# A decoder layer in one core: two late steps of the first MLP half by seven products, and copies of weight sums on another queue

## The chip, the cores and the metric

The kernel runs on one core of a Trainium2 chip. Its time is the device time in microseconds of one execution of the whole layer. Several runs of a kernel are made, and their median is the number that is compared.

## The reference

One layer of a decoder trunk over 1024 tokens of width 1024, with 16 learned tokens put in front of them and dropped at the end. All arrays are float32.

```
u = rmsnorm(h) @ w_in                          # 1024 -> 2048, four pieces of 512
y_lru = rg_lru(conv4(x_lru)) * gelu(g_lru)     # gated linear recurrence
y_cc  = silu(layernorm(conv31(v * sigmoid(g))))
h = h + concat(rmsnorm(y_lru), rmsnorm(y_cc)) @ w_out
m = rmsnorm(h) @ w_mlp_up                      # 1024 -> 4096
h = h + square(relu(m)) @ w_mlp_down           # 4096 -> 1024
out = rmsnorm(h)
```

Most of the matrix products are the MLP's, and it is what the change is about.

## The kernel before

**Products.** A float32 matrix is held as two parts, hi and lo (the rounded value and the rest), both of the type fp32r. Each product is three: hi·hi + hi·lo + lo·hi. For each weight block of 128x1024 the raw block is loaded (512 KB), ACT casts hi (line 313), and DVE subtracts to get lo (line 322). There are 16 buffers for weight blocks in the three forms together, so a load can start only when a block that was used before has been set free.

**Halves.** The tokens are taken in two halves of 512. The mixer of the first half runs first. Then comes the MLP of the first half, with the mixer of the second half worked in between its products; then the MLP of the second half.

**The MLP of the first half** goes in 16 groups of 256 hidden features. `mlp_up` makes 48 matmuls of 128x512 for a group (two blocks of `w_mlp_up`), relu and square on ACT and a subtraction on DVE; `mlp_down` makes 48 more for the group before it (two blocks of `w_mlp_down`), whose sums DVE adds to the residual out of PSUM. Two groups are called a step here; there are eight steps, and the down product of one takes 96 matmuls.

**The MLP of the second half** goes in eight steps of 512 features, each by a scheme of seven products in place of eight (`up_fast`, `down_fast`): the operands are cut in two by two quarters, and sums and differences of the quarters are multiplied. A step's down product takes 84 matmuls in place of 96. For it the activations have to be added and subtracted on DVE, with a further split in hi and lo of each sum. Seven weight blocks go in: three are loaded from the weights, and four are sums of quarters.

**The sums of weights** are made in DRAM by DMAs alone (`weight_sums`). For each step and kind (up, down) there are four blocks, made by four copies from the weights and four DMAs that add onto them. All eight are issued on POOL's queue. There are 15 sums, in the order (step 0, up), (step 0, down), (step 1, up) and so on, without (step 7, down); the last step does its down product another way, by `down_last`. The sums are needed only in the second half.

**What sets the order.** The program is recorded first. Each operation has a duration that the planner assumes, and a list scheduler (`Plan`) then sets one fixed order on every engine, by the priority in which operations were recorded; those recorded under `BG` come last. `tick` hangs one DMA of the sums on every sixth microsecond of planned PE work from 40 on, by an `after` that holds in the plan alone: on the chip no instruction waits for it. POOL thus runs its DMAs as soon as the data that they read are there and POOL gets to them. SP's queue carries x, all weight loads and the stores, in the planned order; where a load must wait for a free buffer, all that stands behind it on SP waits too. DVE and ACT take their instructions in order as well.

**Names of buffers.** `w` is a weight block (raw, hi or lo), `s` a 128x512 slot of activations, `ws_up` and `ws_down` are the sums in DRAM, `mm`, `cv` and `tr` are PSUM banks. In the rows of the order, `ws_up_3_0` is block 0 of the sum for step 3, up.

**Places that the prediction speaks of.** At the start, SP loads x. POOL meanwhile loads blocks of `w_in` with a DMA that adds onto a block that holds minus hi, which makes lo without DVE (`load_split`, line 548). Near 480 us the mixer of the second half and the first half's MLP share PE. From about 560 to 690 us steps 5, 6 and 7 of the first half run; after that the second half's MLP begins. The function that holds the loop over the groups is shown with the others:

Of the kernel before, what the change touches and what calls it, by code (L numbers as in the profile page):

```python
# [14 lines left out]
AF = mybir.ActivationFunctionType  # L15
# [5 lines left out]
KD = D // P  # L21
# [10 lines left out]
NG = NF // 2  # L32
# [30 lines left out]

TABLES = {AF.Sigmoid: 1, AF.Tanh: 2, AF.Exp: 3, AF.Sqrt: 4, AF.Gelu_apprx_tanh: 5, AF.Silu: 6}

G_FIN = 8
G_OUT = 11


class Buf:  # L70
# [204 lines left out]
def hymba_kernel(  # L275
# [25 lines left out]
    def act(o, i, func, scale=1.0, bias=None, accum=None):  # L301
        n = width(i)
        dur = 0.01 + 0.000916 * n + (0.0 if func == AF.Copy else 0.042)
        dur += 0.09 * len(refs(bias, accum)) + 0.115 * len(refs(scale))

        def fn():
            kw = {}
            if bias is not None:
                kw["bias"] = val(bias)
            if accum is not None:  # L310
                kw["accum_out"] = val(accum)
            if func == AF.Copy and isinstance(scale, float) and scale == 1.0:
                nc.scalar.copy(val(o), val(i))  # L313
            else:
                nc.scalar.activation(out=val(o), in_=val(i), func=func, scale=val(scale), **kw)  # L315
        return pl.add("act", dur, fn, refs(i, scale, bias), refs(o, accum), TABLES.get(func))
# [63 lines left out]
    def mms(o, pairs, start=True, stop=True):  # L380

        n = width(o)
        dur = len(pairs) * per_matmul(pairs[0][0], n)
        last = len(pairs) - 1

        def fn():
            for k, (a, b) in enumerate(pairs):
                nc.tensor.matmul(val(o), val(a), val(b), start=start and k == 0,  # L388
                                 stop=stop and k == last)
        rd = [r for p in pairs for r in p]  # L390
        op = pl.add("pe", dur, fn, rd, [o])
        tick(op)
        return op
# [11 lines left out]
    def dma(o, src, nbytes, q="sp", after=()):  # L405
        e = nc.sync if q == "sp" else nc.gpsimd
        return pl.add(q, 0.47 if q == "sp" else 1.02, lambda: e.dma_start(val(o), src), [], [o],
                      nbytes=nbytes, after=after)
# [8 lines left out]
    def dma_pool(o, src, nbytes, add=False, after=()):  # L417
        kw = {"accum_op": ALU.add} if add else {}
        if add and isinstance(src, Ref):
            kw["max_dma_last_dim"] = 1024  # L420
        return pl.add("pool", 1.02, lambda: nc.gpsimd.dma_start(val(o), val(src), **kw),  # L421
                      refs(src) + ([o] if add else []), [o], nbytes=nbytes, after=after)
# [4 lines left out]
    def slot(dt=F32, w=512):  # L427
        return pl.buf("s", dt)[:, 0:w]
# [4 lines left out]
    def bank(tag):  # L433
        return pl.buf(tag)[:, 0:512]
# [93 lines left out]
    def load_cols(w, col):  # L528

        raws = []  # L530
        for h in range(2):
            r = wtile(F32)
            dma(r.view(k4), w[h * 512:(h + 1) * 512, col:col + 256].rearrange("(k p) n -> p k n", p=P),
                1 << 19)
            raws.append(r)
        return raws
# [25 lines left out]
    def prep_win(raws, eng="dve"):  # L562

        return by_column_tile([split_w(r, eng) for r in raws])
# [44 lines left out]
    w_up2 = w_up.rearrange("l d n -> (l d) n")  # L609
# [13 lines left out]
    def weight_sums(q, kind):  # L623

        blk, k, (x, y, z, v) = ((up_block, k4, ((1, 0), (1, 1), (0, 0), (0, 1))) if kind == "up"
                                else (dn_block, k2, ((0, 1), (0, 0), (1, 1), (1, 0))))
        t = [pl.fixed(dr.tile([P, 1024], F32, name=f"ws_{kind}_{q}_{n}"))[:, 0:1024] for n in range(4)]
        n = 1 << 19
        for o, src in ((t[0], x), (t[1], z), (t[2], x), (t[3], v)):
            yield lambda after, o=o, src=src: dma_pool(o.view(k), blk(q, *src), n, after=after)  # L630
        yield lambda after: dma_pool(t[0].view(k), blk(q, *y), n, True, after)
        yield lambda after: dma_pool(t[2].view(k), blk(q, *z), n, True, after)
        yield lambda after: dma_pool(t[1], t[0], n, True, after)
        wsum[q, kind] = t
        yield lambda after: dma_pool(t[3], t[1], n, True, after)

    sums = [(q, kind) for q in range(NG // 2) for kind in ("up", "down")][:-1]

    pace = {"sums": (f for s in sums for f in weight_sums(*s)), "pe": 0.0, "next": SUM_FROM}

# [334 lines left out]
    for c0 in (0, 2):  # L975
        ws = split_win(c0 * P)
# [129 lines left out]
    def mlp_up(gs, u2T, cuts):  # L1106
        ws, bs, hids = {}, {}, []
        for g in gs:
            ws[g] = prep_win(load_cols(w_up2, g * 256))
            bs[g] = [bank("mm"), bank("mm")]  # L1110
        for c0, c1 in cuts:
            for g in gs:
                for j in range(2):
                    pairs = []
                    for k in range(KD):
                        hi, lo = u2T[k]
                        whi, wlo = ws[g][j][k]
                        pairs += [(whi, hi[:, c0:c1]), (whi, lo[:, c0:c1]), (wlo, hi[:, c0:c1])]
                    mms(bs[g][j][:, c0:c1], pairs)
        for g in gs:  # L1120
            hid = []
            for j in range(2):
                r, hi, lo = slot(), slot(F32R), slot(F32R)
                act(r, bs[g][j], AF.Relu)
                act(hi, r, AF.Square)
                act(r, r, AF.Square)
                tt(lo, r, hi.f32, ALU.subtract)
                hid.append((hi, lo))
            hids.append(hid)
        return hids  # L1130

    def mlp_down(gs, hids, hv, done=None, last=False):
        ws = []
        for g in gs:
            for j in range(2):
                r = wtile(F32)
                f0 = (2 * g + j) * P
                dma(r, w_dn2[f0:f0 + P, :], 1 << 19)
                ws.append(split_w(r))
        n = len(ws) - 1  # L1140

        def mm(t, b, c0, c1):
            tsl, dsl = slice(t * P, (t + 1) * P), slice(c0, c1)
            for i, ((hhi, hlo), (whi, wlo)) in enumerate(zip(hids, ws)):
                mms(b, [(hhi[:, tsl], whi[:, dsl]), (hhi[:, tsl], wlo[:, dsl]),
                        (hlo[:, tsl], whi[:, dsl])], start=i == 0, stop=i == n)

        for t in range(4):
            if t == 3 and last:
                last_tile(t, hv, lambda *a: mm(3, *a))  # L1150
                break
            for dh in range(2):
                b = bank("mm")
                mm(t, b, dh * 512, (dh + 1) * 512)
                tt(hv[t][dh], b, hv[t][dh], ALU.add)
            if done is not None:
                done(t)
# [185 lines left out]
    def finish(half, hv):  # L1343
        def done(t):
            r = row_rstd(hv, (t,), rstd_fast if half == 1 else rstd_of)
            for h in range(2):
                o = slot()
                if half == 0 or h == 1:
                    stt(o, hv[t][h], r[:, 0:1], gf[h], ALU.mult, ALU.mult)
                else:  # L1350
                    act(o, hv[t][h], AF.Copy, scale=r[:, 0:1])
                    tt(o, o, gf[h], ALU.mult, "pool")
                put(half, t, h, o)
        return done
# [33 lines left out]
        put(1, t, 1, o1)  # L1388
        put(1, t, 0, o0)

    hB = u2B = None
    todo = []
    for g in range(NG):
        if g < 2:
            if g == 0:
                hids = mlp_up((0, 1), u2A, ((0, 256), (256, 512)))
            hid = hids[g]
        else:
            hid, = mlp_up((g,), u2A, ((0, 512),))
        todo.append((g, hid))  # L1400
        if len(todo) > 1:
            gd, hd = todo.pop(0)
            mlp_down((gd,), hd, hA)
        if g == 5:
            for h in range(2):
                s = slot()
                dma(s, norm_final_g[h * 512:(h + 1) * 512].partition_broadcast(P),
                    1 << 18, "pool", after=[pl.ops[-1]])
                gf.append(s)
        if g == G_FIN:  # L1410
            sqB = slot()
            yB = [lru_y(ct, stB[ct]["h"], sqB) for ct in range(NCT)]
            rlB = sumsq_rstd(sqB)
            ycB, rcB = cc_finish(1)
        if g == G_OUT:
            hBt = [pl.buf("c") for _ in range(4)]
            hB = [[t[:, 0:512], t[:, 512:1024]] for t in hBt]
            load_resid(1, hB, ())
            u2B = out_proj(1, yB, ycB, rlB, rcB, hB)
    u2 = u2_blocks(u2B)  # L1420
    hq = up_fast(0, u2)
    gd, hd = todo.pop(0)
    mlp_down((gd,), hd, hA, finish(0, hA))
    for q in range(1, NG // 2):
        nxt = up_fast(q, u2)
        down_fast(q - 1, hq, hB)
# [36 lines left out]
```

## Time and profile before

| | us |
|---|---|
| median of 3 runs | 1024.62 (1024.51 to 1027.83) |
| the profiled execution | 1022.59 |
| its span (first instruction to last) | 1020.8 |
| TensorE busy in the span | 1002.9 (98%) |
| VectorE busy | 833.1 (82%) |
| ScalarE busy | 524.4 (51%) |
| GpSimd busy | 151.7 (15%) |

The profile is of one execution. PE is the TensorE matmul, PEld its weight load (which runs beside it), DVE VectorE, ACT ScalarE, POOL GpSimd, SP SyncE; SPq is the queue of SP, on which instructions only issue DMAs. In a row, "out<-in" names the buffers, then come the shapes and the number of instructions (x). A bracket or a last column gives the idle time of the engine just before, and behind the arrow what ended it. "PEclk" is the share of its full speed at which TensorE's clock ran in the stretch. "DMA share" is the mean busy share of the 16 DMA engines; it may go slightly above 1.

### The profile page before, as it was taken

The numbers are of one execution on the slowest core, as the hardware profiler recorded it, in microseconds if no ns is written. First come the engines' busy times: TensorE is split into PE (matmuls) and PEld (weight loads), VectorE is DVE, ScalarE is ACT, GpSimd is POOL, SyncE is SP. The second block draws the span as 40 slices with busy tenths as digits, with TensorE's granted clock in tenths as the row PEclk, the third lists the DMA queues.
The fourth block names the chain that finished last, engine by engine and source line by source line (L and its number), as shares of the span: only waits on it lengthen the run. The fifth ranks groups of instructions, "written<-read, shape, count | busy, mean of one in ns | idle before, by whom it ended". The sixth has DMA issues, their size and how long they took to land.

```text
span 1020.8 us, 14830 instructions
## 1 busy us (share of the span) xinstructions
PE 1002.9 (98%) x5624; PEld 864.0 (85%) x5624; DVE 833.1 (82%) x1445; ACT 524.4 (51%) x824; POOL 151.7 (15%) x179
## 2 busy tenths in 40 slices
PE   9999999999999999999899999999999999999997
PEld 7888998988797888878778888889988988989985
DVE  6798898698989999999566575577998797897875
ACT  5831045656678333334353373357666656556644
POOL 4324324212200032222222200000000000000001
PEclk9999999999999999999899999999999999999999
DMA  9449999999922299999999952234856565566522
GB/s 310 101 89 229 194 209 206 212 262 247 225 86 82 83 245 275 243 242 218 246 274 269 212 145 83 97 112 143 282 186 191 177 196 186 177 195 189 183 103 83
DMA packets 113240, 191.19 MB, mean 187 GB/s; under 512 B 6668, under 2 KB 73244, under 8 KB 113168
## 3 DMA queue, kind: packets, MB, share of 16 engines
q0 software_dynamic: 50112, 76.39, 35.4%
q1 hardware_dynamic: 63056, 113.85, 34.1%
q8 instruction: 44, 0.72, 0.3%
q14 instruction: 28, 0.23, 0.1%
HBM read 186.02 MB, written 67.11 MB: 248 GB/s over the span
## 4 chain that ended last, share of the span: by engine, by line
PE 85%; DMA 5%; DVE 4%; ACT 3%; issue 1%; SPq 0%; ACTq 0%
PE mm L388 54%; PE mm L373 17%; PE cv L373 8%; PE tr L373 4%; ACT s L315 2%; DMA s<-in_x_dram 1%; DMA w<-in_w_mlp_down_dram 1%; DVE cv L327 1%; DMA w<-in_w_mlp_up_dram 1%; DVE s L322 1%; PE tr L401 1%; DVE w L322 1%; DMA w<-in_w_out_dram 1%; ACT w L313 1%; DMA w<-in_w_in_dram 1%
## 5 line engine op out<-in xcount | busy, mean ns | idle before, releaser
L388 PE MATMUL mm<-s,w 128*128 128x512 f32 (+2 forms) x2016 | 369.5, 343 | 2.3 <-ACT w L313 1.0
L388 PEld LDWEIGHTS mm<-s,w 128*128 128x128 f32 x2016 | 315.7, 189 | 49.0 <-ACT w L313 1.3
L388 PE MATMUL mm<-w,s 128*128 128x512 f32 (+1 forms) x1260 | 299.2, 395 | 4.3 <-DVE s L322 4.3
L313 ACT CAST w<-w 128x1024 fp32r<-128x1024 f32 x193 | 200.0, 1047 | 193.1 <-DMA w<-in_w_mlp_down_dram 62.0
L388 PEld LDWEIGHTS mm<-w,s 128*128 128x128 f32 x1260 | 235.0, 189 | 59.2 <-DVE s L322 5.8
L322 DVE TENSOR_TENSOR w<-w,w 128x1024 fp32r<-128x1024 f32 x193 | 234.9, 1220 | 55.1 <-ACT w L313 54.5
L327 DVE SCALAR_TENSOR_TENSOR cv<-c,prm,cv 128x512 f32<-128x512 f32 x232 | 162.5, 750 | 0.4
L373 PEld LDWEIGHTS mm<-s,w 128*128 128x128 f32 x1152 | 139.2, 188 | 1.4
L373 PE MATMUL mm<-s,w 128*128 128x256 f32 x1152 | 140.3, 281 | 0.0
L322 DVE TENSOR_TENSOR s<-s,s 128x512 fp32r<-128x512 f32 (+4 forms) x183 | 122.3, 686 | 18.0 <-ACT s L315 15.7
L322 DVE TENSOR_TENSOR s<-mm,s 128x512 f32<-128x512 f32 x144 | 97.6, 686 | 38.5 <-PE mm L388 17.8
L315 ACT ACTIVATE s<-s 128x512 f32<-128x512 f32 (+2 forms) x152 | 95.3, 632 | 33.6 <-DVE s L322 30.7
L373 PE MATMUL cv<-w,s 128*128 128x512 f32 x336 | 83.5, 394 | 0.0
L313 ACT CAST s<-s 128x512 fp32r<-128x512 f32 (+2 forms) x83 | 50.6, 622 | 57.8 <-DVE s L322 40.1
L373 PEld LDWEIGHTS cv<-w,s 128*128 128x128 f32 x336 | 62.2, 188 | 13.7
L322 POOL TENSOR_TENSOR s<-s,s 128x512 f32<-128x512 f32 x3 | 4.6, 1541 | 421.8 <-ACT s L315 421.8
L421 POOL DMA_DIRECT2D ws_up<-in_w_mlp_up_dram x48 | 48.5, 1279 | 47.3 <-DMA ws_up<-in_w_mlp_up_dram 47.3
L313 ACT COPY s<-mm 128x512 f32<-128x512 f32 (+2 forms) x48 | 24.4, 513 | 60.2 <-PE mm L373 32.1
L421 POOL DMA_DIRECT2D ws_down<-in_w_mlp_down_dram x42 | 39.6, 1251 | 56.8 <-DMA ws_down<-in_w_mlp_down_dram 56.8
L322 DVE TENSOR_TENSOR c<-mm,c 128x512 f32<-128x512 f32 (+2 forms) x49 | 31.0, 634 | 14.4 <-PE mm L388 14.0
L315 ACT ACTIVATE s<-mm 128x512 f32<-128x512 f32 x40 | 23.7, 594 | 34.0 <-PE mm L388 33.3
L373 PE MATMUL mm<-w,s 128*128 128x512 f32 x168 | 41.1, 393 | 0.0
(133 smaller groups left out, 718.3 us busy)
## 6 DMA issues: line engine op xcount, KB each, us to landing
w<-in_w_mlp_down_dram SPq DMA_DIRECT2D x57, 512.0 KB, 4.3
w<-in_w_mlp_up_dram SPq DMA_DIRECT2D x56, 512.0 KB, 4.8
ws_up<-in_w_mlp_up_dram POOLq DMA_DIRECT2D x48, 512.0 KB, 9.4
ws_down<-in_w_mlp_down_dram POOLq DMA_DIRECT2D x42, 512.0 KB, 9.4
w<-ws_up SPq DMA_DIRECT2D x32, 512.0 KB, 3.9
w<-ws_down SPq DMA_DIRECT2D x28, 512.0 KB, 4.0
w<-in_w_in_dram POOLq DMA_DIRECT2D x24, 512.0 KB, 8.4
ws_up<-ws_up POOLq DMA_DIRECT2D x16, 512.0 KB, 7.8
```

Source lines behind the costliest of these rows:

```text
L313: nc.scalar.copy(val(o), val(i))
L315: nc.scalar.activation(out=val(o), in_=val(i), func=func, scale=val(scale), **kw)
L322: return pl.add(eng, dur, lambda: e.tensor_tensor(out=val(o), in0=val(a), in1=val(b), op=op), refs(a, b), [o])
L327: return pl.add("dve", dur, lambda: nc.vector.scalar_tensor_tensor(out=val(o), in0=val(a), scalar=val(s), in1=val(b), op0=op0, op1=op1), r ...
L373: nc.tensor.matmul(val(p), val(a), val(b), start=start and i == 0 and k == 0, stop=k == len(pairs) - 1, skip_group_check=True)
L388: nc.tensor.matmul(val(o), val(a), val(b), start=start and k == 0, stop=stop and k == last)
L401: nc.tensor.transpose(val(o), val(i), ident.real[:rows, :rows])
L421: return pl.add("pool", 1.02, lambda: nc.gpsimd.dma_start(val(o), val(src), **kw), refs(src) + ([o] if add else []), [o], nbytes=nbytes, a ...
```

## The change

There are four edits.

1. `FAST = (5, 6)`: steps 5 and 6 of the first half take their down product by `down_fast`, as the second half does. Their up product stays at 96 matmuls (`up_blocks`), and its output is evacuated in pieces of 128x256, since `down_fast` needs quarters by tokens.
2. The sums for (step 5, down) and (step 6, down) are made first, since they are now used in the first half.
3. The four copies of each sum go by `dma` (SP's queue) in place of `dma_pool`. The DMAs that add stay on POOL.
4. The loop runs over steps instead of groups. The second half's mixer is finished after step 4 (before: in the middle of step 4, after group 8), and its output projection is made after step 5 (group 11, as before).

```diff
-G_FIN = 8
-G_OUT = 11
+Q_FIN = 4
+Q_OUT = 5
+FAST = (5, 6)
@@ weight_sums
         for o, src in ((t[0], x), (t[1], z), (t[2], x), (t[3], v)):
-            yield lambda after, o=o, src=src: dma_pool(o.view(k), blk(q, *src), n, after=after)
+            yield lambda after, o=o, src=src: dma(o.view(k), blk(q, *src), n, after=after)
         yield lambda after: dma_pool(t[0].view(k), blk(q, *y), n, True, after)
...
-    sums = [(q, kind) for q in range(NG // 2) for kind in ("up", "down")][:-1]
+    sums = [(q, "down") for q in FAST]
+    sums += [s for q in range(NG // 2) for s in ((q, "up"), (q, "down"))
+             if s not in sums and s != (NG // 2 - 1, "down")]
...
+    def up_blocks(q, u2T):
+        h = {(t, i): slot() for t in range(2) for i in range(2)}
+        for i in range(2):
+            ws = prep_win(load_cols(w_up2, q * 512 + i * 256))
+            for j in range(2):
+                b = bank("mm")
+                pairs = []
+                for k in range(KD):
+                    hi, lo = u2T[k]
+                    whi, wlo = ws[j][k]
+                    pairs += [(whi, hi), (whi, lo), (wlo, hi)]
+                mms(b, pairs)
+                for t in range(2):
+                    act(h[t, i][:, j * 256:(j + 1) * 256], b[:, t * 256:(t + 1) * 256], AF.Relu)
+        return h
...
+    for q in range(NG // 2):
+        if q in FAST:
+            todo.append(("fast", q, up_blocks(q, u2A)))
+            down_next()
+        else:
+            for g in (2 * q, 2 * q + 1):
...
+                todo.append(("plain", g, hid))
+                if len(todo) > 1:
+                    down_next()
...
-        if g == G_FIN:
+        if q == Q_FIN:
...
-        if g == G_OUT:
+        if q == Q_OUT:
...
-    gd, hd = todo.pop(0)
-    mlp_down((gd,), hd, hA, finish(0, hA))
+    if NG // 2 - 1 in FAST:
...
+    else:
+        down_next(finish(0, hA))
```

`down_next` takes the next entry of the list and calls `mlp_down` for a plain group or `down_fast(q, h, hA)` for a fast step.

In numbers of instructions: on PE there are 24 matmuls of 128x512 fewer. DVE has 6 more subtractions of weight blocks, 14 more of activations and 4 fewer evacuations of PSUM; ACT has 6 more casts of weight blocks, 14 more casts of activations, 8 fewer squares, 8 fewer relus of 128x512 and 16 more of 128x256. SP has 6 more loads of weight blocks (512 KB each) and the 60 copies that POOL no longer issues.

**SP's queue at the start.** Before, the last loads of x are followed by the first weight block of the output projection:

```order
L407 DMA s_44_297<-in_x_dram 128x512
L407 DMA s_45_304<-in_x_dram 128x512
L407 DMA s_48_313<-in_x_dram 128x512
L407 DMA s_51_323<-in_x_dram 128x512
L407 DMA s_53_331<-in_x_dram 128x512
L407 DMA w_211_1690<-in_w_out_dram 128x2x512
```

In the changed kernel eight copies stand in between:

```order
L409 DMA s_51_323<-in_x_dram 128x512
L409 DMA s_53_331<-in_x_dram 128x512
L409 DMA ws_down_6_3_92<-in_w_mlp_down_dram 256x1x512
L409 DMA ws_down_5_1_86<-in_w_mlp_down_dram 256x1x512
L409 DMA ws_down_5_0_85<-in_w_mlp_down_dram 256x1x512
L409 DMA ws_down_5_2_87<-in_w_mlp_down_dram 256x1x512
L409 DMA ws_down_5_3_88<-in_w_mlp_down_dram 256x1x512
L409 DMA ws_down_6_0_89<-in_w_mlp_down_dram 256x1x512
L409 DMA ws_down_6_1_90<-in_w_mlp_down_dram 256x1x512
L409 DMA ws_down_6_2_91<-in_w_mlp_down_dram 256x1x512
L409 DMA w_211_1690<-in_w_out_dram 128x2x512
L409 DMA w_222_1766<-in_w_out_dram 128x2x512
```

These are the copies of the two sums for the first half's fast steps. They read the weights and write DRAM, so they wait for no buffer.

**SP's queue near 480 us.** Before, pairs of up and down blocks of the first half alternate:

```order
L407 DMA w_704_4630<-in_w_mlp_down_dram 128x1024
L407 DMA w_707_4660<-in_w_mlp_down_dram 128x1024
L407 DMA w_717_4721<-in_w_mlp_up_dram 128x4x256
L407 DMA w_719_4725<-in_w_mlp_up_dram 128x4x256
L407 DMA w_732_4804<-in_w_mlp_down_dram 128x1024
L407 DMA w_736_4847<-in_w_mlp_down_dram 128x1024
L407 DMA w_750_4920<-in_w_mlp_up_dram 128x4x256
L407 DMA w_752_4927<-in_w_mlp_up_dram 128x4x256
```

In the changed kernel, from the same loads on:

```order
L409 DMA w_704_4630<-in_w_mlp_down_dram 128x1024
L409 DMA w_707_4660<-in_w_mlp_down_dram 128x1024
L409 DMA w_717_4721<-in_w_mlp_up_dram 128x4x256
L409 DMA w_719_4725<-in_w_mlp_up_dram 128x4x256
L409 DMA ws_up_3_0_117<-in_w_mlp_up_dram 512x1x256
L409 DMA w_732_4804<-in_w_mlp_up_dram 128x4x256
L409 DMA w_735_4833<-in_w_mlp_up_dram 128x4x256
L409 DMA ws_up_3_1_118<-in_w_mlp_up_dram 512x1x256
L409 DMA w_746_4891<-in_w_mlp_down_dram 128x1024
L409 DMA ws_up_3_2_119<-in_w_mlp_up_dram 512x1x256
L409 DMA w_749_4904<-in_w_mlp_down_dram 128x1024
```

The four copies of one sum stand among the loads, one behind every one or two of them; POOL no longer issues them.

**SP's queue in the second half.** Before, weight blocks and finished sums of one step alternate:

```order
L407 DMA w_1193_7237<-in_w_mlp_down_dram 128x2x512
L1179 DMA w_1197_7246<-ws_down_0_3_92 128x1024
L407 DMA w_1200_7257<-in_w_mlp_up_dram 128x4x256
L1179 DMA w_1203_7280<-ws_up_2_0_101 128x1024
L1179 DMA w_1207_7302<-ws_up_2_1_102 128x1024
L407 DMA w_1214_7330<-in_w_mlp_up_dram 128x4x256
L1179 DMA w_1218_7352<-ws_up_2_2_103 128x1024
L1179 DMA w_1222_7375<-ws_up_2_3_104 128x1024
```

In the changed kernel the copies of a sum for a later step stand among them:

```order
L1200 DMA w_1210_7269<-ws_down_0_3_100 128x1024
L409 DMA w_1214_7290<-in_w_mlp_up_dram 128x4x256
L409 DMA ws_up_6_2_139<-in_w_mlp_up_dram 512x1x256
L1200 DMA w_1222_7320<-ws_up_2_0_109 128x1024
L1200 DMA w_1225_7339<-ws_up_2_1_110 128x1024
L409 DMA ws_up_6_3_140<-in_w_mlp_up_dram 512x1x256
L409 DMA w_1233_7376<-in_w_mlp_up_dram 128x4x256
L1200 DMA w_1236_7390<-ws_up_2_2_111 128x1024
L1200 DMA w_1242_7424<-ws_up_2_3_112 128x1024
L409 DMA w_1246_7456<-in_w_mlp_up_dram 128x4x256
L409 DMA w_1258_7505<-in_w_mlp_down_dram 128x2x512
L1200 DMA w_1261_7535<-ws_down_1_0_105 128x1024
```

Here the copies of (step 6, up) stand ahead of loads for steps 2 and 1. From the first fast step on, 20 copies stand among the loads in this manner.

## Rows read from the trace of the kernel before

**Rows 1.** The page, part 1: busy us (share of the span) and instructions.

```profile
PE 1002.9 (98%) x5624; PEld 864.0 (85%) x5624; DVE 833.1 (82%) x1445; ACT 524.4 (51%) x824; POOL 151.7 (15%) x179
```

**Rows 2.** The page, part 5: count, busy us, mean ns, idle before.

```profile
L388 PE MATMUL mm<-w,s 128*128 128x512 f32 (+1 forms) x1260 | 299.2, 395 | 4.3 <-DVE s L322 4.3
```

**Rows 3.** Busy time by stretch; columns in the first row, an x count behind each.

```profile
core 0: us, PE busy (x) PEld busy (x) DVE busy (x) ACT busy (x) POOL busy (x), PEclk, DMA share, GB/s
...
490.00:495.00 5.00, 1.98 (x9) 1.33 (x8) 2.29 (x5) 1.04 (x1) 0.82 (x1) 0.88 1.08 225
495.00:500.00 5.00, 5.00 (x13) 3.84 (x13) 4.79 (x16) 1.04 (x1) 1.06 (x1) 0.50 0.71 112
...
500.00:580.00 80.00, 79.99 (x363) 64.69 (x362) 45.19 (x67) 32.96 (x46) 21.68 (x24) 1.00 1.06 272
600.00:680.00 80.00, 80.00 (x356) 65.07 (x355) 46.64 (x70) 34.45 (x52) 0.00 (x0) 1.00 0.31 99
690.00:800.00 110.00, 110.00 (x724) 100.47 (x724) 100.06 (x172) 72.53 (x108) 0.00 (x0) 1.00 0.60 198
```

**Rows 4.** Timeline 465 to 530 us: start, length, engine, what; in brackets the idle time before.

```profile
477.10 3.20 POOL L421 DMA_DIRECT2D ws_down<-in_w_mlp_down_dram  x4
...
478.79 2.94 SPq L407 DMA_DIRECT2D w<-in_w_mlp_up_dram  x2
...
491.63 1.04 ACT L313 CAST w<-w 128x1024 fp32r<-128x1024 f32 x1 [6.32 <-DMA w<-in_w_mlp_up_dram]
492.71 1.22 DVE L322 TENSOR_TENSOR w<-w,w 128x1024 fp32r<-128x1024 f32 x1 [5.04 <-ACT w L313]
...
494.66 5.49 PE L388 MATMUL mm<-w,s 128*128 128x512 f32 x12 [3.02 <-DVE s L322]
...
503.19 3.14 POOL L421 DMA_DIRECT2D ws_up<-in_w_mlp_up_dram  x4
```

**Rows 5.** Chain that ended last, in order of time: start, length, what.

```profile
606.43 77.89 PE mm L388 x336
...
777.30 2.80 PE mm L373 x12
```

**Rows 6.** DMA issues of 380 to 585 us: KB each, median us from issue to landing.

```profile
w<-in_w_mlp_down_dram SPq DMA_DIRECT2D x13, 512.0 KB, 6.7
w<-in_w_mlp_up_dram SPq DMA_DIRECT2D x12, 512.0 KB, 7.3
```

**Rows 7.** DMA issues of 600 to 680 us, same columns.

```profile
w<-in_w_mlp_up_dram SPq DMA_DIRECT2D x7, 512.0 KB, 3.7
```

**Rows 8.** DMA issues of 690 to 800 us, same columns.

```profile
w<-ws_up SPq DMA_DIRECT2D x12, 512.0 KB, 3.9
...
w<-in_w_mlp_down_dram SPq DMA_DIRECT2D x7, 512.0 KB, 4.4
```

**Rows 9.** All instructions on the sums of up weights: their DMAs.

```profile
DMA to landing us min/median/max: 3.1/7.7/14.1
```

**Rows 10.** Groups of 770 to 990 us: busy us, mean ns, idle before.

```profile
L322 DVE TENSOR_TENSOR w<-w,w 128x1024 fp32r<-128x1024 f32 x78 | 95.1, 1220 | 9.6 <-ACT w L313 9.6
...
L313 ACT CAST w<-w 128x1024 fp32r<-128x1024 f32 x78 | 80.1, 1046 | 13.4 <-DVE w L322 9.0 <-DMA w<-in_w_mlp_up_dram 4.0 <-DMA w<-in_w_mlp_down_dram 0.2
...
L322 DVE TENSOR_TENSOR s<-s,s 128x512 fp32r<-128x512 f32 (+1 forms) x59 | 39.1, 684 | 0.7 <-ACT s L313 0.6
```

**Rows 11.** Timeline of the SP queue, 9 to 150 us.

```profile
9.49 14.25 SPq L407 DMA_DIRECT2D s<-in_x_dram  x8
141.32 4.59 SPq L407 DMA_DIRECT2D w<-in_w_out_dram  x2
```

**Rows 12.** Timeline of POOL, 28 to 56 us.

```profile
44.66 1.32 POOL L421 DMA_DIRECT2D w<-in_w_in_dram  x1 [13.13 <-ACT w L315]
48.50 1.29 POOL L421 DMA_DIRECT2D w<-in_w_in_dram  x1 [2.53 <-ACT w L315]
```

**Rows 13.** Timeline of PE, 50 to 60 us.

```profile
52.44 7.88 PE L388 MATMUL mm<-s,w 128*128 128x512 f32 x44
```

More of the change, by code (lines that the diff above doesn't have):

```diff
@@ L1389, in last_tile, with down_next @@
         put(1, t, 0, o0)
-    hB = u2B = None
+    hB = u2B = hq = None
     todo = []
[L1393 to L1397, printed above, removed]
-        else:
-            hid, = mlp_up((g,), u2A, ((0, 512),))
-        todo.append((g, hid))
-        if len(todo) > 1:
-            gd, hd = todo.pop(0)
-            mlp_down((gd,), hd, hA)
-        if g == 5:
+    def down_next(done=None):
+        k, i, h = todo.pop(0)
+        if k == "plain":
+            mlp_down((i,), h, hA, done)
+        else:
+            down_fast(i, h, hA)
+    for q in range(NG // 2):
[4 more added lines that the diff above has]
+            for g in (2 * q, 2 * q + 1):
+                if g < 2:
+                    if g == 0:
+                        hids = mlp_up((0, 1), u2A, ((0, 256), (256, 512)))
+                    hid = hids[g]
+                else:
+                    hid, = mlp_up((g,), u2A, ((0, 512),))
+                todo.append(("plain", g, hid))
+                if len(todo) > 1:
+                    down_next()
+        if q == 2:
             for h in range(2):
@@ L1421, in hymba_kernel @@
     hq = up_fast(0, u2)
-    gd, hd = todo.pop(0)
-    mlp_down((gd,), hd, hA, finish(0, hA))
+    if NG // 2 - 1 in FAST:
+        down_next()
+        done = finish(0, hA)
+        for t in range(4):
+            done(t)
+    else:
+        down_next(finish(0, hA))
     for q in range(1, NG // 2):
```

## The prediction

> **What bounds the kernel now.** I read the page first. TensorE is busy 1002.9 of 1020.8 us, 98% of the span [rows 1]; no other engine comes near. So the time is the number of matmuls by their duration, and 17.9 us in which PE has nothing, or runs its matmuls slowly on top of that. The groups of instructions say what PE waits for: in the products that have weights as the stationary side it waited 4.3 us, all of it for DVE making slots of activations [rows 2].
>
> The windows by stretch and the timeline show where most of that stands. In 490 to 495 us PE is busy 1.98 of 5 us, and in 495 to 500 the granted clock is 0.50, the lower of TensorE's two levels (1.2 of 2.4 GHz) [rows 3]. The timeline gives the chain. POOL issues four copies of a sum at 477.10, two loads of up weights are issued behind them on SP at 478.79; the cast of the block that had to come starts at 491.63, 12.8 us after that issue, when ACT has been idle for 6.32 us; DVE then subtracts from 492.71 after 5.04 us of idle time; and PE, after 3.02 us without work, runs 12 matmuls in 5.49 us [rows 4]. PE was idle first and slow afterwards: that stall costs more than its idle time.
>
> The list of DMA issues shows that this is a crowded stretch: weight blocks of 512 KB land 6.7 and 7.3 us after their issue in 380 to 585 us [rows 6], 3.7 us in 600 to 680 us [rows 7], when POOL issues nothing. In 500 to 580 the DMA engines are busy at 1.06, in 600 to 680 at 0.31 [rows 3].
>
> **The change part by part.** *Fewer matmuls.* The plain products are 336 matmuls in 77.89 us, 0.2318 us each; a product of the scheme is 12 in 2.80, 0.233 each [rows 5]. So nothing is lost by the other form, and 2 × (96 − 84) = 24 fewer save 24 × 0.2318 = 5.6 us. This is on the path as long as PE is the bound in the two steps. It lies in a stretch where PE is busy 79.99 and 80.00 of 80 us [rows 3].
>
> *DVE and ACT in the two steps.* DVE gets 6 × 1.220 = 7.3 us for weight blocks and 14 × 0.684 = 9.6 us for slots [rows 10], 16.9 us (4 evacuations fewer are left out). Its free time is 80 − 45.2 = 34.8 us in 500 to 580 and 33.4 in 600 to 680 [rows 3], 68 together. ACT gets 6 × 1.046 = 6.3 us for weight blocks [rows 10], and at most 1.046 each for 14 casts and 8 relus of half that size or less, 23 us more; its free time is 47.0 + 45.6 = 93 us [rows 3]. Both cost nothing on the path. If that cover were gone, PSUM would be read late and PE would wait for a bank; the second half shows the same scheme at work with DVE busy 100.06 of 110 us, and PE still at 110.00 [rows 3]. For the same reason I put the six extra loads (512 KB each, into a stretch with the DMA engines at 0.31) and the relus by 128x256 at nothing. The finish of the second half's mixer comes later by half a step; it is work beside the products in 500 to 580, where PE has no idle time: nothing.
>
> *Copies off POOL's queue near 480 us.* Today POOL issues four copies at once, and the DMAs that add behind them; one sum runs from 477.10 to the next four at 503.19, 26.1 us [rows 4], one after another as fast as the data allow. In the changed order the four copies of one sum stand one by one behind loads on SP, and the two loads that were late (the second and third of the fences on this place) stand ahead of all four. POOL's adding DMAs then come when their copies have landed, so the burst is spread. I take the stall away: 3.02 idle, and 5.49 − 12 × 0.2318 = 2.7 for the slow matmuls, 5.7 us. Bounds: nothing, if other DMAs take the place of the burst, and 5.7. PE's other waits for DVE are 4.3 − 3.0 = 1.3 us [rows 2]; I take 0.5 of them, bounds 0 and 1.3.
>
> *Copies among the loads later.* Before, POOL is silent in 600 to 680 and 690 to 800 us (busy 0.00) [rows 3]; the sums are finished. Now SP's order really paces them, and 20 copies stand among the loads from the first fast step on. SP issues them in order and waits only for buffers, but a load behind a copy shares its way. The trace has no copy on SP's queue. From below: nothing, since the engines are at 0.31 and 0.60 of their time [rows 3] and blocks land in 3.7 to 4.4 us [rows 7, 8]. From above: each of the 20 holds the load behind it for a whole copy, whose shortest landing is 3.1 us [rows 9], and PE has one product in hand, 2.80 less the 0.684 of a DVE operation, 2.1 us; so 1.0 us each, 20 us. I take 2.5 us, near the lower end, since ACT waited for weights only 4.0 + 0.2 us in 770 to 990 [rows 10]: the loads are issued well ahead of use.
>
> *Eight copies at the start.* SP has issued x by 9.49 + 14.25 = 23.7 us and its next DMA comes at 141.32 [rows 11], so its queue is empty, and no weight load stands behind the copies for long. At 3.1 us each they run to about 49 us. POOL issues loads with addition at 44.66 and 48.50 [rows 12], and PE uses weights from 52.44 on [rows 13]. If the copies slow these two loads by one copy each, 6.2 us, less the 0.8 us between 48.50 + 3.1 and 52.44, PE waits 5 us; at best nothing. I take 0.5, since most copies will have landed before the first of the two is issued.
>
> The sum: −5.6 − 5.7 − 0.5 + 2.5 + 0.5 = −8.8. Against the profiled execution, 1022.59 us (span 1020.8 and 1.8 around it), that is 1013.8. The median of the runs shown, 1024.62, stands 2.03 above that execution, so the median of the changed kernel comes to 1015.8.
>
> **The rivals.** *The stall stays or moves (R1).* The sums are the same bytes, and 12.8 us of landing came with the DMA engines at 1.08 [rows 3, 4]; if it is the crowd of bytes and not their order, another load will be late in 380 to 585 us. For it: the landing follows the share of the engines, 6.7 us at 1.06, 3.7 at 0.31 [rows 3, 6, 7]. Against it: many loads at the same share hurt nobody; the one that did was behind four copies issued at once. Then the two relief terms fall away: −5.6 + 2.5 + 0.5 = −2.6, 1022.0. The Trainium skill, "DMA: Bandwidth & Descriptors", section "Issuing engines are not separate DMA queues", says that DMAs of all engines run on the same 16 engines and that issuing from several saves only the issuing time; by that rule R1 is what happens, and the trace agrees with it so far as landing goes with the share.
>
> *Copies in the weights' queue cost more than they free (R2, slower).* The place is the second half, 690 us and after. A load behind a copy lands late; ACT's cast waits, DVE's subtraction behind it, and the evacuations of PSUM that are queued behind the subtraction on DVE; PE then has no bank. That is the stall of 490 us, in small, 20 times. For it: DVE is busy 91% there (100.06 of 110) [rows 3], with little to catch up by. Against it: blocks land within 4.4 us today [rows 8]. At 1.0 us a copy: 1024.6 − 5.6 − 5.7 + 20 = 1033.3. It breaks even at 11.3 / 20 = 0.57 us a copy and is slower by more than 0.5% from (11.3 + 5.1) / 20 = 0.82. The Trainium skill, "DMA: Bandwidth & Descriptors", section "Queues, rings and completion order", says that an engine drains each ring in order and takes turns between the rings by packets; by it a load on SP's ring waits for the whole copy ahead, where behind a copy on POOL's ring it would have had every other turn. No run here shows a copy and a load on one ring.
>
> *The start (R3).* The eight copies delay the loads of `w_in`, PE waits the 5 us worked out above: 1015.8 + 4.5 = 1020.3. For it: the margin is 0.8 us; against it: the time in which the copies can be done.
>
> That the change doesn't do what it says (the fast steps wait for their sums) I give nothing of its own: those sums are the first to be made, eight copies and eight adding DMAs, at 26.1 us a sum, and the steps that use them lie after 500 us.
>
> **How the numbers follow.** About 5.1 us (0.5%) is what a measurement here can tell from no change, so faster means under 1019.5 and slower over 1029.7. Forecast: 57%, its own range 1010.5 to 1019.5 (relief of waits 5.7 + 1.3 and copies at nothing gives 1012.0, a little faster clock after it the rest; copies at 6 us give the upper end). R1 21%, 1022.0; R2 13%, 1033.3; R3 9%, 1020.3. Faster: most of the forecast (0.54), a quarter of R1 (R1 with copies at nothing is 1019.5) and a few of R3's, 0.60. Slower: R2 but for its cheap cases, and a little of the others, 0.13. The rest, 0.27, is no change. The range 1010 to 1026 leaves out R2's 13% and a few per cent below.
>
> **What would show it right or wrong.** After the change the timeline should have PE without a gap at 478 to 500 us and the clock at 1.00 there; 84 matmuls (19.6 us) for each of the two down products; weights landing in less than 6.7 us in 380 to 585; PE's busy time in 600 to 800 still full. Under R1 a gap with a low clock stands elsewhere in the first 600 us. Under R2, PE's idle time behind DVE grows after 560 us, with casts that wait for a DMA of weights. Under R3 PE idles between 44 and 60 us. The forecast falls if PE's busy time does not sink by about 5.6 us (then matmuls are slower in the two steps), or if idle time beyond 5 us appears anywhere that has none today.

## The result, and the profile after

The changed kernel takes 1010.67 us (1007.43 to 1011.15, 4 runs), the kernel before 1025.88 (1024.51 to 1027.83, 4 runs): a ratio of 0.9846, with an interval of 0.9821 to 0.9871, that is 13.2 to 18.4 us less. The profiled execution took 1011.15 us, against 1022.59 before: 11.4 less. I had forecast 1015.8, and 8.8 us less, between the medians as between the profiled executions.

The first two rows of the page that matter, and what answers to [rows 1, 2]:

```profile
PE 994.4 (99%) x5600; PEld 857.6 (85%) x5600; DVE 845.2 (84%) x1461; ACT 534.1 (53%) x844; POOL 106.6 (11%) x119
...
L390 PE MATMUL mm<-w,s 128*128 128x512 f32 (+1 forms) x1068 | 251.5, 393 | 0.7 <-DVE s L324 0.7
```

PE is busy 1002.9 − 994.4 = 8.5 us less. That is 24 × 0.2318 = 5.6 for the matmuls and 2.7 for the twelve slow ones of the stall [rows 4]: 8.3. Its idle time in the span falls from 17.9 to 15.0 us; behind DVE in the products of the second row, from 4.3 [rows 2] to 0.7. Busy time by stretch, columns as in [rows 3], first of the kernel before where the earlier rows don't show it:

```profile
20.00:60.00 40.00, 37.54 (x273) 35.00 (x272) 31.29 (x97) 28.32 (x58) 10.81 (x15) 0.96 0.59 155
140.00:300.00 160.00, 157.65 (x980) 138.94 (x979) 130.95 (x284) 97.15 (x179) 36.85 (x40) 1.00 0.88 213
380.00:480.00 100.00, 99.21 (x438) 79.73 (x437) 98.00 (x148) 34.81 (x45) 27.52 (x31) 1.00 0.97 239
```

And of the changed kernel:

```profile
20.00:60.00 40.00, 35.09 (x262) 32.80 (x261) 27.97 (x90) 27.60 (x57) 9.14 (x13) 0.96 0.84 237
140.00:300.00 160.00, 160.00 (x998) 141.78 (x997) 133.85 (x290) 99.09 (x182) 15.06 (x14) 1.00 0.69 165
380.00:480.00 100.00, 100.00 (x432) 80.77 (x432) 99.08 (x141) 35.38 (x46) 9.79 (x10) 1.00 0.73 189
490.00:495.00 5.00, 5.00 (x36) 4.02 (x35) 4.49 (x16) 0.59 (x1) 1.01 (x1) 1.00 1.10 279
500.00:580.00 80.00, 79.79 (x372) 64.33 (x371) 50.75 (x102) 40.32 (x73) 5.31 (x5) 1.00 0.66 184
600.00:680.00 80.00, 80.00 (x380) 66.33 (x379) 69.18 (x94) 41.36 (x58) 5.31 (x5) 1.00 0.83 231
690.00:800.00 110.00, 109.31 (x715) 99.28 (x714) 98.71 (x172) 72.31 (x107) 9.79 (x9) 1.00 0.98 284
```

Read the first number after the length (PE busy) and the last but one (DMA share). PE's gaps went in three places: 3.0 us in 490 to 495, 0.8 in 380 to 480, and 2.35 in 140 to 300, which I had not counted. They came in two: 2.45 us more in 20 to 60, 0.7 in 690 to 800 (and 0.2 in 500 to 580). The DMA engines are less busy in 140 to 300, 380 to 480 and 500 to 580 us and busier from 600 to 800.

The DMA issues of 380 to 585 us (KB each, median us to landing), for [rows 6], and of 690 to 800, for [rows 8]:

```profile
w<-in_w_mlp_up_dram SPq DMA_DIRECT2D x14, 512.0 KB, 4.7
...
w<-in_w_mlp_down_dram SPq DMA_DIRECT2D x10, 512.0 KB, 3.9
```

```profile
w<-ws_up SPq DMA_DIRECT2D x10, 512.0 KB, 7.1
w<-in_w_mlp_down_dram SPq DMA_DIRECT2D x9, 512.0 KB, 5.7
```

Weight blocks land in 4.7 and 3.9 us where they took 7.3 and 6.7, and in 5.7 to 7.1 us where they took 3.9 to 4.4. The traffic has moved to a stretch where PE loses only 0.7 us. Timeline of the changed kernel near 480 us:

```profile
477.15 0.34 SPq L409 DMA_DIRECT2D w<-in_w_mlp_down_dram  x1
477.54 0.56 SPq L409 DMA_DIRECT2D ws_up<-in_w_mlp_up_dram  x1
...
479.71 0.34 SPq L409 DMA_DIRECT2D w<-in_w_mlp_down_dram  x1
479.75 11.29 PE L390 MATMUL mm<-w,s 128*128 128x512 f32 x48
...
482.09 1.05 ACT L315 CAST w<-w 128x1024 fp32r<-128x1024 f32 x1 [0.21 <-DMA w<-in_w_mlp_down_dram]
```

A copy is issued 0.4 us behind a load; the cast starts 4.9 us after the first load's issue (12.8 before [rows 4]), ACT waited 0.21 us for it, and PE runs on. The fast step's down product begins with the first and ends behind the last of these rows of PE's timeline:

```profile
599.70 2.94 PE L375 MATMUL cv<-w,s 128*128 128x512 f32 x12
...
616.42 2.93 PE L375 MATMUL cv<-w,s 128*128 128x512 f32 x12
619.19 11.29 PE L390 MATMUL mm<-s,w 128*128 128x512 f32 x48
```

That is 619.19 − 599.70 = 19.5 us for 84 matmuls, as in the second half, with nothing idle.

At the start, the rows of POOL, ACT and PE in the changed kernel's timeline:

```profile
31.36 1.53 POOL L409 DMA_DIRECT2D w<-in_w_in_dram  x2 [1.53 <-DVE ty L338]
```

```profile
45.35 1.06 ACT L317 ACTIVATE w<-w 128x1024 fp32r<-128x1024 f32 x1 [4.32 <-DMA w<-in_w_in_dram]
```

```profile
48.19 0.63 PE L403 MATMUL cv<-ident,s 128*128 128x128 f32 x4 [3.00 <-DVE s L329]
```

ACT stood 4.32 us before a block of `w_in`, one of two that POOL had loaded from 31.36 on, beside the copies on SP. Behind that instruction on ACT stand the evacuations of the transposes, DVE's come after them, and PE waited 3.00 us. It is rival R3, but the late load is the plain one and ACT the engine that blocks, not the loads with addition (44.66 and 48.50 us before [rows 12]).

### The profile page after: what moved, and what is told of

Its sections match the earlier page's. It is cut to its first block, busy times and chain, and to the rows that moved or that the text cites. A ratio compares the mean times of both kernels' runs of the same rounds, so it can differ in the third digit from the quotient of the medians.

```text
span 1009.4 us, 14861 instructions
## 1 busy us (share of the span) xinstructions
PE 994.4 (99%) x5600; PEld 857.6 (85%) x5600; DVE 845.2 (84%) x1461; ACT 534.1 (53%) x844; POOL 106.6 (11%) x119
## 3 DMA queue, kind: packets, MB, share of 16 engines
q0 software_dynamic: 41472, 44.93, 27.7%
## 4 chain that ended last, share of the span: by engine, by line
PE 87%; DVE 4%; DMA 4%; ACT 3%; issue 1%; POOL 1%; POOLq 0%; ACTq 0%
PE mm L390 54%; PE mm L375 17%; PE cv L375 10%; PE tr L375 4%; DMA w<-in_w_in_dram 3%; DVE s L324 2%; ACT s L317 2%; PE tr L403 1%; DVE s L329 1%; PE tr L390 1%; DVE w L324 1%; DMA s<-in_out_norm_lru_g_dram 0%; PE cv L403 0%; ACT w L315 0%; DVE s L353 0%
## 5 line engine op out<-in xcount | busy, mean ns | idle before, releaser
L390 PE MATMUL mm<-w,s 128*128 128x512 f32 (+1 forms) x1068 | 251.5, 393 | 0.7 <-DVE s L324 0.7
L324 DVE TENSOR_TENSOR s<-s,s 128x512 fp32r<-128x512 f32 (+4 forms) x197 | 131.8, 691 | 11.0 <-ACT s L317 5.3
L375 PE MATMUL cv<-w,s 128*128 128x512 f32 x432 | 107.1, 395 | 0.0
L324 DVE TENSOR_TENSOR s<-mm,s 128x512 f32<-128x512 f32 x120 | 82.3, 693 | 25.6 <-PE mm L390 10.9
L375 PEld LDWEIGHTS cv<-w,s 128*128 128x128 f32 x432 | 80.3, 188 | 17.9
L315 ACT CAST s<-s 128x512 fp32r<-128x512 f32 (+2 forms) x97 | 59.3, 621 | 60.4 <-DVE s L324 42.0
L375 PE MATMUL mm<-w,s 128*128 128x512 f32 x216 | 53.0, 394 | 0.0
L423 POOL DMA_DIRECT2D ws_up<-in_w_mlp_up_dram x16 | 18.6, 1164 | 264.4 <-DMA ws_up<-in_w_mlp_up_dram 253.1
L317 ACT ACTIVATE s<-mm 128x512 f32<-128x512 f32 (+1 forms) x48 | 24.3, 523 | 37.8 <-PE mm L390 37.5
L423 POOL DMA_DIRECT2D ws_down<-in_w_mlp_down_dram x14 | 15.8, 1267 | 177.6 <-DMA ws_down<-in_w_mlp_down_dram 177.6
```

What stands on the lines that cost most here:

```text
L324: return pl.add(eng, dur, lambda: e.tensor_tensor(out=val(o), in0=val(a), in1=val(b), op=op), refs(a, b), [o])
L375: nc.tensor.matmul(val(p), val(a), val(b), start=start and i == 0 and k == 0, stop=k == len(pairs) - 1, skip_group_check=True)
```

## The experiments

Each was timed in rounds beside the kernel before, whose medians in the three groups were 1027.12, 1026.83 and 1025.93 us. Ratios are to it; lengths in us are the ratio's distance from 1 times that median.

**The copies alone.** The kernel before, with

```diff
-            yield lambda after, o=o, src=src: dma_pool(o.view(k), blk(q, *src), n, after=after)
+            yield lambda after, o=o, src=src: dma(o.view(k), blk(q, *src), n, after=after)
```

> The kernel before, with one edit: the four copies of each sum go by SP's queue. No fast step in the first half, sums in the old order. Theory A (copies in a burst on POOL make weight blocks late): the gap at 490 us and its slow matmuls go (5.7 us), and the small gaps between 140 and 480 us too (up to 3 us); a new wait near 45 us, of 3 us, comes as in the changed kernel; so 5 to 7 us less than before, about 1020 (ratio 0.994). Rival B (the whole gain is in the fast steps; the stall only lies elsewhere because work moved): within 2 us of before, about 1025 (0.999), with a gap of 2 us or more and a clock near 0.5 somewhere in 380 to 600 us.

Measured: 1012.77 us (1011.96 to 1014.59), ratio 0.9873 (0.9845 to 0.9901): 13.0 us less, twice what theory A gave. The stall at 490 us and the gaps in 140 to 300 are gone; 0.8 us are still lost in 380 to 480:

```profile
140.00:300.00 160.00, 160.00 (x995) 141.47 (x994) 133.41 (x288) 99.80 (x182) 15.06 (x14) 1.00 0.68 168
380.00:480.00 100.00, 99.16 (x440) 79.47 (x440) 97.21 (x149) 36.27 (x48) 9.80 (x10) 1.00 0.71 181
490.00:495.00 5.00, 5.00 (x23) 4.06 (x22) 4.22 (x7) 0.17 (x1) 1.01 (x1) 1.00 1.10 284
```

So B falls, and most of the whole gain comes from this one edit. The wait of 3 us near 45 us, which the expectation had, did not come: PE is busy 37.80 us in 20 to 60, with eight copies on SP there as well. PE's whole busy time is 1000.0 us, 2.9 below the kernel before and 5.6 above the changed kernel: the slow matmuls (2.7 us) went with the copies, the 24 matmuls with the fast steps.

**All but the copies.** The changed kernel with `dma` turned back to `dma_pool` in that line.

> The changed kernel with the copies back on POOL's queue; the fast steps and the order of the sums stay. Theory A: only the 24 matmuls are saved, and the late blocks come back: 4 to 6 us less than before, about 1020 (ratio 0.995), weights landing in 6.5 us or more in 380 to 585 us, a gap of PE of some us with slow matmuls behind it, no wait near 45 us. Rival B: like the changed kernel, about 1011 (0.985), without a gap.

Measured: 1021.33 us (1013.63 to 1027.23), ratio 0.9941 (0.9911 to 0.9971): 6.1 us less, which holds the 5.6 us of 24 matmuls. This and the copies alone add up to 19.1 us, more than the 13.2 to 18.4 of both; by the medians of different rounds, the fast steps make the kernel with copies on SP only 2.1 us shorter (1012.77 to 1010.67), or 4.1 with the changed kernel's second time (1008.7, below). Of what is missing, 1.7 to 2.5 us is the wait at the start (what PE lost in 20 to 60 us in the two traces of the changed kernel), which neither of these two runs has. The profiled execution was a long one (1027.23 us) and shows what the copies on POOL do: windows, DMA issues of 380 to 585, and one row of PE's timeline.

```profile
140.00:300.00 160.00, 154.75 (x911) 134.67 (x911) 123.54 (x274) 90.42 (x167) 37.18 (x41) 0.97 0.86 205
380.00:480.00 100.00, 96.17 (x404) 76.03 (x403) 92.06 (x132) 30.76 (x41) 26.11 (x29) 0.98 1.00 248
```

```profile
w<-in_w_mlp_up_dram SPq DMA_DIRECT2D x14, 512.0 KB, 7.2
w<-in_w_mlp_down_dram SPq DMA_DIRECT2D x10, 512.0 KB, 8.7
```

```profile
453.64 7.15 PE L390 MATMUL mm<-w,s 128*128 128x512 f32 x24 [2.48 <-DVE s L324]
```

PE lost 5.25 us in 140 to 300 and 3.8 in 380 to 480; in the profile of the kernel before, the large gap stood at 490 us instead. Where the gaps fall differs between these two traces, and the time differs between executions: these 12 runs spread over 13.6 us, and the 39 of the kernel before that ran beside the experiments over 14.1 (1019.15 to 1033.23), against 2.6 for the five with the copies on SP. With copies on SP the other groups of five or six below spread over 1.1 to 6.1 us.

**The first copies.** The changed kernel with

```diff
+        cp = dma_pool if kind == "down" and q in FAST else dma
         for o, src in ((t[0], x), (t[1], z), (t[2], x), (t[3], v)):
-            yield lambda after, o=o, src=src: dma(o.view(k), blk(q, *src), n, after=after)
+            yield lambda after, o=o, src=src: cp(o.view(k), blk(q, *src), n, after=after)
```

> The changed kernel with only the eight copies of the first two sums on POOL, where they stand behind the loads of w_in; all others on SP. PE, DVE and ACT have the same order as in the changed kernel. If the eight copies on SP right behind x cause the wait of 3.0 us near 45 us (loads of w_in landing in 13.2 us instead of 7.9), that wait goes and so does the time at half clock behind it: 2.5 us less than the changed kernel, about 1008 (0.982). Rival: the loads of w_in are late by themselves in that layout of the start, and the wait stays: 1010.7.

Measured: 1009.94 us (1009.42 to 1010.54), ratio 0.9841 (0.981 to 0.9872). The transposes of the row at 48.19 above, and the row ahead of them, in PE's timeline:

```profile
44.01 3.08 PE L390 MATMUL mm<-s,w 128*128 128x256 f32 x24
46.93 0.60 PE L403 MATMUL cv<-ident,s 128*128 128x128 f32 x4
```

The wait of 3.00 us is gone, so the eight copies do make it. But they are not enough for it: with the copies alone, and with three fast steps below, eight copies run there on SP and PE is busy 37.80 and 38.16 us in 20 to 60. And taking them away brings no gain that can be told from none: PE is busy 36.72 us in 20 to 60 (35.09 above), but 158.89 of 160 in 140 to 300, one wait for another.

**The changed kernel again**, for its time in the second group and another trace.

> The changed kernel once more, for its time beside the next three kernels and a second trace of its start. The second trace settles whether the 3.0 us wait near 45 us belongs to the kernel. If it does, about 1011 with the wait; if it is one execution's accident, about 1010 to 1011 and 20 to 60 us shows PE busy for 36.5 us or more of 40, as with the copies alone on SP (37.80).

Measured: 1008.7 us (1007.97 to 1009.62), ratio 0.983 (0.9788 to 0.9872). PE was busy 35.88 us in 20 to 60, with a wait of 1.7 us where the first trace had 3.0. The wait belongs to the kernel; its size changes. Its median lies 2 us under that of the first four runs.

**Paced on POOL.** The changed kernel with each copy on POOL, held back by a marker:

```diff
+    def paced(o, src, n, after):
...
+        d = pl.add("dve", 0.06, lambda: nc.vector.memset(m, 0.0), [], [mk[:, i:i + 1]], after=after)
...
+        p = pl.add("pool", 0.06, lambda: nc.gpsimd.memset(m, 0.0), [], [mk[:, i:i + 1]], after=[d])
+        dma_pool(o, src, n, after=[p])
```

> The changed kernel with all copies on POOL, but each copy held back until VectorE has come to the place in its program at which the plan put the copy: VectorE writes one column, POOL overwrites it and then issues the copy (60 such pairs, some 60 ns each on VectorE). Theory A1 (POOL runs ahead of the plan, and its burst crowds the weights): late blocks go although the copies stay on POOL: about 1011 (ratio 0.985), spread of the runs 4 us or less. Theory A2 (POOL's queue itself is what hurts the weights' loads, whenever it is used): as with the copies back on POOL, about 1021 (0.994), spread 10 us.

Measured: 1013.56 us (1011.76 to 1015.8), ratio 0.9878 (0.9839 to 0.9917): 12.5 us less. Issues of 380 to 585, and a window:

```profile
w<-in_w_mlp_up_dram SPq DMA_DIRECT2D x14, 512.0 KB, 4.7
w<-in_w_mlp_down_dram SPq DMA_DIRECT2D x11, 512.0 KB, 5.2
```

```profile
140.00:300.00 160.00, 157.84 (x971) 138.40 (x970) 128.90 (x294) 95.51 (x176) 22.89 (x37) 0.99 0.58 147
```

A1 holds for the larger part: on the same queue, held to the plan, the copies cost 6.4 us less than free ones (12.5 against 6.1 us under the kernel before), and the spread is 4 us. But 4.9 us remain against the copies on SP (1008.7), in runs that don't overlap. Part of it is a gap at 160 us with slower matmuls behind it: between the same two matmuls PE takes 34.5 us (134.66 to 169.18) where the second trace of the changed kernel takes 30.5 (136.86 to 167.32). The rest stays open; the markers, 3.5 us of DVE's time in all, are part of this run too.

**A faster pace.** `SUM_EVERY = 4.4` in place of 6.0.

> The changed kernel with one DMA of the sums at every 4.4 us of planned PE work instead of 6, so that SP's copies come as often as POOL came to them before (120 DMAs from 49 to 585 us, 4.5 us each). If the mean amount of traffic in 140 to 585 us is what makes weights late: gaps of PE return in that stretch, 1014 to 1018. If it is the run of several copies at once: no gap there, and the 0.7 us gap at 690 to 770 us goes, since the copies end earlier: 1009 to 1011.

Measured: 1010.46 us (1008.06 to 1014.02), ratio 0.985 (0.9809 to 0.989). Three windows, and a row of PE's timeline:

```profile
140.00:300.00 160.00, 157.60 (x978) 138.87 (x977) 130.34 (x285) 96.53 (x178) 19.35 (x18) 1.00 0.79 186
380.00:480.00 100.00, 100.00 (x432) 80.93 (x431) 98.96 (x142) 34.70 (x45) 12.87 (x13) 1.00 0.87 215
...
690.00:800.00 110.00, 110.00 (x725) 100.45 (x724) 99.77 (x173) 72.29 (x107) 0.00 (x0) 1.00 0.60 197
```

```profile
161.73 0.39 PE L390 MATMUL tr<-s,gw_a_hi 128*128 128x272 f32 x1 [1.50 <-ACT s L315]
```

Both expectations came half true: the gap behind 690 us went, one near 160 us came, and the time is the same within the spread. The gap near 160 us can't be put down to the pace alone: a smaller one, 1.1 us in all, stands there in the traces of the kernel before and of the first copies on POOL. In 380 to 480 PE is busy 100.00 of 100 us with 22 DMAs of the sums issued, against 17 in the changed kernel. That is not yet POOL's old rate there, which was 31, so what that rate would do on SP is not shown.

**Four at once.**

```diff
-        for o, src in ((t[0], x), (t[1], z), (t[2], x), (t[3], v)):
-            yield lambda after, o=o, src=src: dma(o.view(k), blk(q, *src), n, after=after)
+        yield lambda after: [dma(o.view(k), blk(q, *src), n, after=after)
+                             for o, src in ((t[0], x), (t[1], z), (t[2], x), (t[3], v))]
+        for _ in range(3):
+            yield lambda after: None
```

> The changed kernel with the four copies of a sum handed to the planner at one place, every 48 us, instead of one after another, 6 us apart; all still on SP. If four copies at once make the loads behind them late, whatever the queue: weights behind them land in 12 us and more, PE has gaps with slow matmuls, 1014 to 1020. If it takes POOL's queue for that (a burst on another queue beside the loads): as the changed kernel, 1010 to 1012.

Measured: 1009.63 us (1008.31 to 1012.22), ratio 0.9842 (0.9803 to 0.9881). Issues and window of 690 to 800:

```profile
w<-ws_up SPq DMA_DIRECT2D x10, 512.0 KB, 13.2
...
w<-in_w_mlp_up_dram SPq DMA_DIRECT2D x7, 512.0 KB, 13.2
```

```profile
690.00:800.00 110.00, 109.02 (x710) 98.25 (x709) 98.74 (x171) 70.87 (x107) 8.71 (x8) 1.00 0.94 274
```

Loads behind four copies do land in 13.2 us instead of about 7, and PE loses 0.3 us more. So here lateness alone costs little; I take it that these loads are issued far enough ahead.

**Three fast steps.** `FAST = (5, 6, 7)`.

> The changed kernel with step 7 by seven products as well (12 matmuls fewer, one more sum made at the start, four more copies behind x). If PE stays the bound in the step: 12 x 0.232 = 2.8 us less, less up to 1.5 us for a longer wait at the start: about 1009 (0.983). Rival: DVE, with 8.5 us more in a stretch that leads into the second half, makes PE wait, and the store of the first half is no longer overlapped tile by tile: 1011 or more, with PE idle behind DVE between 640 and 720 us.

Measured: 1015.36 us (1010.56 to 1016.67), ratio 0.9884 (0.9854 to 0.9913): slower than two, as far as the groups tell (the first copies on POOL, timed in the same rounds, 1009.42 to 1010.54; the first four runs of the changed kernel overlap with these a little). The row of PE's timeline, and DVE's just before:

```profile
661.34 10.06 PE L375 MATMUL mm<-s,w 128*128 128x256 f32 x70 [3.70 <-DVE w L324]
```

```profile
660.06 1.22 DVE L324 TENSOR_TENSOR w<-w,w 128x1024 fp32r<-128x1024 f32 x1
```

**Three fast steps at the faster pace**, to tell whether traffic or DVE made that wait.

> Steps 5, 6 and 7 by seven products, and one DMA of the sums at every 4.4 us of planned PE work instead of 6, so that fewer copies are left for 600 to 770 us. With three fast steps at the old pace PE waited 3.7 us for a subtraction of a weight block on DVE near 661 us. Theory D (DVE is full there, and the subtraction stands behind those of the activations): the gap near 660 us stays at 3 to 4 us: 1011 to 1015. Rival T (the traffic of late copies, DMA engines at 0.99 in 690 to 770 us, made the block late): the gap shrinks below 1 us, and three fast steps win their 2.8 us: 1006 to 1008, the fastest so far.

Measured: 1016.72 us (1014.72 to 1019.66), ratio 0.9892 (0.9867 to 0.9918).

```profile
669.20 11.19 PE L375 MATMUL mm<-s,w 128*128 128x256 f32 x70 [3.69 <-DVE w L324]
```

The wait is the same, 3.69 us, with the DMA engines at 0.46 in 660 to 690. DVE runs without a pause from 662 to 669 us there, and its subtraction of the weight block stands behind ten of activations. Theory D holds for the wait; the step next to the second half has no free DVE. The time, 1016.72, lies above the 1011 to 1015 expected under it. The matmuls behind the wait run slower too: the mean granted clock in 660 to 690 us is 0.94 with three fast steps and 0.89 here, against 1.00 with two.

No variant beats the changed kernel beyond the spread of runs.

## Why the prediction was right, and where it was off

- *Fewer matmuls, 5.6 us.* Right: 6.1 (3.0 to 9.1) with the copies on POOL; PE is busy 5.6 us less than with the copies alone; and 84 matmuls took 19.5 us.
- *DVE, ACT and six loads at nothing.* Right in steps 5 and 6: PE is busy 80.00 of 80 in 600 to 680 with DVE at 69.18. The price if the cover is gone is what the third fast step showed, 3.7 us of waiting, and slower matmuls, against 2.8 won. In 500 to 580 us PE lost 0.2 us behind DVE; every trace with fast steps has that or more, and the copies alone (79.99 of 80) don't.
- *Copies off POOL's queue, 5.7 + 0.5 us.* The mechanism was right, the size was not: 13.0 us (10.2 to 15.9) by itself. So this is the term that was mis-sized. I took one profiled execution's gaps as the kernel's. It was one of the shorter ones; beside the stall I counted only PE's waits in one kind of product, 1.3 us; the gaps in 140 to 300 us stood outside that, 2.35 in that trace and 5.25 in another with the copies on POOL. Adding 2.03 us to come from execution to median was the same mistake: what differs between executions is mostly this very term, and with the copies on SP the spread falls from 14.1 us to 2.6.
- *Copies among the loads, +2.5 us.* Less: 0.7 us of PE in 690 to 800, where "still full" had been a sign of being right. R2's price of 1.0 us a copy did not come, although blocks land up to 7.1 us after their issue there, and 13.2 behind four copies.
- *The start, +0.5 us.* Too small: PE lost 2.45 us in one trace and about 1.7 in the other. R3's mechanism was there in half its size: with those copies on POOL the wait is gone. That the copies alone and three fast steps have none, with eight copies there too, I can't explain.
- *R1* fell: with the same bytes on SP the gaps go. Its evidence held, though: landing goes with the share of the DMA engines (0.73 and 4.7 us after, 0.97 and 7.3 before). What changed is that share: POOL's adding DMAs now last into the second half (9.79 us of POOL in 690 to 800, nothing before). SP paces them, a copy there waiting its turn behind loads that wait for buffers: between 400 and 480 us each copy, or pair of copies, is issued within 0.1 us of the end of the load's issue ahead of it. The longest wait of SP's queue in the changed kernel, for PE to be done with buffers (us in total, times, longest):

```profile
SPq L409 <- PE mm L390: 435.9, 59, 114.2
```

That the pacing is what helps is shown by the paced runs: free copies on POOL 6.1 us under the kernel before, paced ones 12.5. Why the paced ones stay 4.9 us behind SP is not.

The range held the time near its lower end, 0.67 us inside it, because the largest term was twice its size and the start took part of it back. That was luck in part: two errors offset each other, and the changed kernel's second group of runs has its median at 1008.7, below the range.

## What to carry to other kernels

Background DMAs on a queue that runs free go as fast as the data allow, whatever place the plan gave them; put them on a queue whose order paces them, and look where the traffic then goes. When runs of a kernel spread by more than a per cent and the profile shows one stall, don't price the cause from that execution alone: the stall cost 5.7 us here, and moving the copies brought 13.0. Before cutting PE's work at DVE's cost, look at each step's own DVE time: two steps here had it to spare, the next had not.

## What the runs showed of the hardware

The DMA queues, from the page (packets, MB, share of 16 engines' span), before and after:

```profile
q0 software_dynamic: 50112, 76.39, 35.4%
q1 hardware_dynamic: 63056, 113.85, 34.1%
```

```profile
q1 hardware_dynamic: 89200, 148.46, 44.1%
q0 software_dynamic: 41472, 44.93, 27.7%
```

The copies took 31.46 MB off POOL's queue and 35.4% of 1020.8 − 27.7% of 1009.4 = 82 us of the engines' time, 2.6 us per MB; SP's queue got 34.61 MB (with six loads) and 97 us, 2.8 per MB. These are differences between two traces, so estimates; by them a copy is no dearer on POOL. What is left there, mostly DMAs that add, beside loads of `w_in`, takes 280 us for 44.93 MB, 6.2 per MB: more than twice as much in these traces.
